# Convolution with max-pooling on one core: another order of warm-ups, weight turns and loads in the head

## The chip, the cores and the metric

The kernel runs on one core of one Trainium2 chip. The metric is the device time of a whole execution in microseconds. Profile times count from the first instruction of the profiled execution.

## What is computed

A 3x3 convolution with zero padding over 16 images of 64 channels and 64x64 pixels, 128 output channels, then the maximum over 2x2 blocks of pixels. Input, weights and output are fp32.

```python
x_pad = np.pad(x, ((0, 0), (0, 0), (1, 1), (1, 1)))
conv[b, co] += weight[co, ci, kh, kw] * x_pad[b, ci, kh:kh+h, kw:kw+w]   # over ci, kh, kw
output[b, c, i, j] = np.max(conv[b, c, 2*i:2*i+2, 2*j:2*j+2])
```

## The kernel before

**Tiles.** Two images at a time lie on the 128 partitions (2 x 64 channels). Every product in `taps` uses one image, so 64 partitions of input and a 64x128 weight, and products for the two images run in pairs. Eight pairs of images are split into two classes: four pairs "k" are cast to bf16 and multiplied as they are (`kx`); four pairs "w" are loaded in fp32 (`wx`) and enter as sums and differences of neighbouring rows. Each pair is cut into four chunks of 16 rows; unit i stands for chunk i % 4 of pair i // 4, and there are 16 units in each class. A unit gives 8 rows of the pooled output for two images.

**Two rows at once.** For each pair of output rows the kernel computes one PSUM tile `ta` and one `tb`. For class k: PA(i) fills `ta` (12 products with the weights D2 and G0), PB(i) fills `tb` (12 with D0 and G2). EV(i) copies `ta` to SBUF on ScalarE, MX(i) takes the maximum of the two into `tb` on VectorE, and PR(i) adds to `tb` the products of G1 with the row sums KS(i), which both rows share. OD(i) copies the odd columns on ScalarE, CM(i) takes the maximum with the even ones on VectorE and stores. For class w the parts are P2, P0 (into `ta`), SE (ScalarE puts minus `ta` into `tb`), P3, P1 (into `tb`) and ev, mx, od, cm; their inputs are the row operations E (`we`), Z (`wz`), Y (`wy`) and WS (`ws`). KS, WS and the first five E run on VectorE, Z and Y on GpSimd. There are four PSUM tiles of two banks each (`acc`), handed out by the list `free` in the order of the program.

**Weights.** `wraw` holds the raw weights. Seven blocks of them are needed with input channels on the partitions: D2 = g2-g1, G0, D0 = g0-g1, G2, GM, G1 and GP, with GM and GP half of g0+g2-g1 and half of g0+g2+g1. Each is made as a bf16 block of `wq` (VectorE or ScalarE), turned by four transposes on TensorE into a PSUM tile (TD2, TG0, ...; `turn`, line 148), and copied to `wt` (VD2, VG0, ...; `turn_out`, lines 161 to 167). GS, the sum g0+g2, runs on GpSimd.

**Order.** Nothing is scheduled automatically: each engine gets its instructions in the order of the strings HEAD, STEADY and TAIL, and does them in that order. `behind` adds a wait of one instruction for another; `on_gpsimd` lets a GpSimd operation wait for the last VectorE operation noted by `on_vector`.

**The head.** Before HEAD, eight products of zeros warm up TensorE (`zero`, line 135; two for each PSUM tile[...]). The loads go out from SyncE's queue: `wraw` and `kfirst` (the first 17 rows of the first k pair) at once, the first `wx` chunk behind the fourth warm-up, and after it `ksecond` (the next 16 rows). XO casts the odd rows of `kfirst` on VectorE, XE the even ones; X1 and X2 do the same for `ksecond` on ScalarE. The other three `wx` chunks wait for XO. The remaining rows of the first k pair are loaded from GpSimd's queue with a cast under way (`kload`, line 95), behind E.0. A tile in the set `unset` gets two products of zeros when SE first uses it.

Of the kernel before, what the change touches and what calls it, by code (L numbers as in the profile page):

```python
# [11 lines left out]
def kernel(  # L12
# [21 lines left out]
    nc = tc.nc  # L34
    FP32 = mybir.dt.float32
    BF16 = mybir.dt.bfloat16
    MAX = mybir.AluOpType.max
    ADD = mybir.AluOpType.add
    SUB = mybir.AluOpType.subtract

    B, CI, H, W = x.shape
# [18 lines left out]

    acc = [psum.tile([128, 2, R, W], FP32, name=f"acc_{i}") for i in range(4)]
    free = deque(range(4))
    unset = set()

# [3 lines left out]
    def behind(inst, other):  # L70
        if other is not None:
            tc.add_manual_dep(inst.ins, other.ins.name, SYNC, reason="order")

    def on_vector(inst):
        sbuf_op[0] = inst
        return inst

    def on_gpsimd(inst):
        behind(inst, sbuf_op[0])
        return inst  # L80


    def rows_of(p, lo, hi):
        return x[2 * p : 2 * p + 2].rearrange("b c h w -> (b c) h w")[:, lo:hi, :]

    def chunk(q):
        return (2 * R * q + (q > 0), min(H, 2 * R * (q + 1) + 1))
# [4 lines left out]
    def kload(j, lo, hi):  # L92
        if j not in kx:
            kx[j] = kx_pool.tile([128, H, W], BF16, name="kx")
        return nc.gpsimd.dma_start(out=kx[j][:, lo:hi, :], in_=rows_of(2 * j, lo, hi))  # L95

    def wload(i):
        j, q = divmod(i, NQ)
        lo, hi = chunk(q)
        return nc.sync.dma_start(  # L100
            out=wx[j % 2][:, lo + 1 : hi + 1, :], in_=rows_of(2 * j + 1, lo, hi)
        )
# [6 lines left out]
    klo2, khi2 = chunk(1)  # L109
    ksecond = const.tile([128, khi2 - klo2, W], FP32)  # L110
# [10 lines left out]
    D2, G0, D0, G2, GM, G1, GP = range(1, 29, 4)  # L121
    BLOCKS = {"D2": D2, "G0": G0, "D0": D0, "G2": G2, "GM": GM, "G1": G1, "GP": GP}
# [6 lines left out]
    g0, g1, g2 = wv[:, 0:3, :], wv[:, 3:6, :], wv[:, 6:9, :]  # L129

    def slots(m):
        return wq[:, m : m + 3, :]

    def zero(t, h):
        return nc.tensor.matmul(  # L135
            acc[t][:, h], zeros[:, 0:128], zeros, start=True, stop=True, skip_group_check=True
        )

    turned = {}

    def turn(m):
        t = free.popleft()
        turned[m] = t
        unset.add(t)
        tp = acc[t][:, 0].rearrange("p a b -> p (a b)").bitcast(BF16)
        lo, hi = BLOCKS[m] - 1, BLOCKS[m] + 3
        for j in range(lo, hi):
            nc.tensor.transpose(  # L148
                tp[:, (j - lo) * 128 : (j - lo + 1) * 128],
                wq[:, j : j + 2, :].rearrange("a b c -> a (b c)"),  # L150
                ident,
            )

    def turn_out(m):
        t = turned[m]
        free.append(t)
        lo, hi = BLOCKS[m] - 1, BLOCKS[m] + 3
        src = acc[t][:, 0].rearrange("p a b -> p (a b)").bitcast(BF16)[:, 0 : (hi - lo) * 128]
        dst = wt[:, lo:hi, :].rearrange("p a b -> p (a b)")
        if m == "GM":  # L160
            nc.scalar.mul(dst, src, 0.5)
        elif m == "GP":
            nc.vector.tensor_scalar_mul(out=dst, in0=src, scalar1=0.5)
        elif m in ("G0", "G1", "G2"):
            nc.scalar.copy(out=dst, in_=src)
        else:
            nc.vector.tensor_copy(out=dst, in_=src)
# [66 lines left out]
    def row_out(name, i):  # L234
        j, q = divmod(i, NQ)
        if (name, j) not in row:
            row[name, j] = row_pool.tile([128, HO, W], BF16, name=name)
        return row[name, j][:, q * R : (q + 1) * R, :]

    def row_in(t, first, pad):  # L240
        a = first + pad
        return t[:, a : a + 2 * R - 1 : 2, :]

    def row_op(engine, name, i, a, b, op):
        j, q = divmod(i, NQ)
        t, pad = (kx[j], 0) if name == "ks" else (wx[j % 2], 1)
        f = 2 * R * q
        return engine.tensor_tensor(  # L248
            out=row_out(name, i), in0=row_in(t, f + a, pad), in1=row_in(t, f + b, pad), op=op
        )  # L250

    def ks(i):
        on_vector(row_op(nc.vector, "ks", i, 0, 1, ADD))

    def ws(i):
        on_vector(row_op(nc.vector, "ws", i, 0, 1, ADD))

    def we(i):
        if i < 5:
            inst = on_vector(row_op(nc.vector, "we", i, 1, 0, SUB))  # L260
            if i == 0:
                behind(kload(0, chunk(2)[0], H), inst)
        else:
            on_gpsimd(row_op(nc.gpsimd, "we", i, 1, 0, SUB))

# [69 lines left out]
    def cast_rows(first):  # L335
# [3 lines left out]
        if first == 1:  # L339
            for i in range(1, NQ):  # L340
                behind(wload(i), inst)

    def cast_more(first):
        nc.scalar.copy(out=kx[0][:, klo2 + first : khi2 : 2, :], in_=ksecond[:, first::2, :])

# [2 lines left out]
        "g1": lambda: nc.scalar.copy(out=slots(G1), in_=g1),  # L348
        "g2": lambda: nc.scalar.copy(out=slots(G2), in_=g2),
        "D2": lambda: on_vector(nc.vector.tensor_sub(out=slots(D2), in0=g2, in1=g1)),  # L350
        "D0": lambda: on_vector(nc.vector.tensor_sub(out=slots(D0), in0=g0, in1=g1)),
        "GS": lambda: on_gpsimd(nc.gpsimd.tensor_tensor(out=gsum, in0=g0, in1=g2, op=ADD)),
        "GM": lambda: on_vector(
            nc.vector.tensor_sub(out=slots(GM), in0=gsum, in1=g1)
# [4 lines left out]
        "XO": lambda: cast_rows(1),  # L359
        "XE": lambda: cast_rows(0),  # L360
        "X1": lambda: cast_more(0),
        "X2": lambda: cast_more(1),
        "PA": pa, "PB": pb, "PR": pr, "P0": p0, "P1": p1, "P2": p2, "P3": p3,
        "KS": ks, "WS": ws, "E": we, "Z": wz, "Y": wy, "SE": seed,
        "EV": lambda i, h=None: evac(("k", i), h), "ev": lambda i, h=None: evac(("w", i), h),
        "MX": lambda i, h=None: rowmax(("k", i), h), "mx": lambda i, h=None: rowmax(("w", i), h),
# [3 lines left out]
    for m in BLOCKS:  # L370
        steps["T" + m] = lambda m=m: turn(m)
        steps["V" + m] = lambda m=m: turn_out(m)

    HEAD = """
        D2 g0 D0 g2 GS g1 TD2 VD2 TG0 VG0 XO TD0 VD0 TG2 VG2 TG1 VG1 XE GM PA.0 GP TGM VGM TGP
        KS.0 E.0 WS.0 PB.0 EV.0 X1 Z.0 Y.0 VGP P2.0 MX.0 SE.0 X2 PA.1 EV.1 WS.1 KS.1 E.1 PR.0
        P0.0 P3.0 Z.1 Y.1 OD.0 CM.0 P2.1 ev.0 PB.1 SE.1 mx.0 P0.1 P1.0 MX.1 P3.1 ev.1 od.0 PR.1
        WS.2 KS.2 E.2 Z.2 Y.2 OD.1 cm.0 CM.1 PA.2 EV.2 P2.2 PB.2 SE.2 mx.1 P1.1 P0.2 MX.2 P3.2
        od.1 ev.2 cm.1 E.3 KS.3 WS.3 Z.3 Y.3 PR.2 PA.3 OD.2 CM.2 P2.3 mx.2 EV.3 PB.3 SE.3 P1.2
# [12 lines left out]
    """  # L392
    FIRST, LAST = 4, 12

    for n in range(8):
        warm = zero(n // 2, n % 2)
        if n == 3:
            behind(wload(0), warm)
            nc.sync.dma_start(out=ksecond, in_=rows_of(0, klo2, khi2))
    kx[0] = kx_pool.tile([128, H, W], BF16, name="kx")  # L400

    def run(order):
# [44 lines left out]
```

## Time and profile before

| | us |
|---|---|
| median of 4 runs (107.57 to 108.78) | 107.98 |
| the profiled execution | 107.94 |
| its span, first to last instruction | 106.2 |
| TensorE busy | 98.9 |
| VectorE busy | 82.6 |
| ScalarE busy | 72.7 |
| GpSimd busy | 60.2 |

The span is that of one execution; the time of the same execution holds 1.7 us more. In the profile PE is TensorE, PEld its weight loads, DVE VectorE, ACT ScalarE, POOL GpSimd and SP SyncE; a letter q behind a name is the engine's queue. A line such as "L183" is the kernel's line, and since helpers issue most instructions, the tiles tell more than the lines: `acc<-kx,wt` at L183 is PA or PB, `acc<-we,wt` is P2, `acc<-ident,wq` at L148 a turn. The chain of waits goes back from the last instruction to what released each step. The timeline has, on each line, the start, the length, the engine, the line and operation, the tiles and their shape, how many instructions are merged, and in brackets the idle time before them and what ended it.

### The profile page before, as it was taken

The numbers are of one execution on the slowest core, as the hardware profiler recorded it, in microseconds if no ns is written. First come the engines' busy times: TensorE is split into PE (matmuls) and PEld (weight loads), VectorE is DVE, ScalarE is ACT, GpSimd is POOL, SyncE is SP. The second block draws the span as 40 slices with busy tenths as digits, with TensorE's granted clock in tenths as the row PEclk, the third lists the DMA queues.
The fourth block names the chain that finished last, engine by engine and source line by source line (L and its number), as shares of the span: only waits on it lengthen the run. The fifth ranks groups of instructions, "written<-read, shape, count | busy, mean of one in ns | idle before, by whom it ended". The sixth has DMA issues, their size and how long they took to land.

```text
span 106.2 us, 2338 instructions
## 1 busy us (share of the span) xinstructions
PE 98.9 (93%) x900; PEld 45.4 (43%) x900; DVE 82.6 (78%) x113; ACT 72.7 (68%) x92; POOL 60.2 (57%) x69
## 2 busy tenths in 40 slices
PE   5989989999999999999999999999999999999810
PEld 2445434444444444444444444444444444455400
DVE  1489989969797869698787868687978868686950
ACT  4557985676767678767867676787777676775820
POOL 6205674823519494958567594949294765835000
PEclk9999999999999999999999999999999999999995
DMA  2998996899986768999956589999968412232052
GB/s 63 346 342 275 318 208 146 213 267 328 277 301 177 223 158 158 215 331 201 336 210 193 194 190 158 237 319 208 364 220 176 150 68 102 99 105 99 0 198 99
DMA packets 12475, 21.96 MB, mean 207 GB/s; under 512 B 944, under 2 KB 9136, under 8 KB 12464
## 3 DMA queue, kind: packets, MB, share of 16 engines
q1 hardware_dynamic: 11312, 18.03, 53.3%
q0 software_dynamic: 1008, 3.65, 19.3%
q8 instruction: 7, 0.11, 0.4%
q10 hardware_dynamic: 144, 0.13, 0.4%
q14 instruction: 4, 0.03, 0.1%
HBM read 17.07 MB, written 8.39 MB: 240 GB/s over the span
## 4 chain that ended last, share of the span: by engine, by line
PE 80%; DVE 10%; DMA 4%; issue 1%; ACT 1%; SPq 0%; DVEq 0%
PE acc L183 80%; DVE acc L299 6%; DMA kfirst<-in_x_dram 4%; DVE ws L248 2%; DVE o L318 1%; DVE we L248 1%; ACT od L304 1%; PE acc L148 1%; DVE kx L337 0%; SPq L105 0%; DVE ks L248 0%; DVEq L299 0%
## 5 line engine op out<-in xcount | busy, mean ns | idle before, releaser
L183 PEld LDWEIGHTS <-wt 64*128 64x128 bf16 x864 | 42.6, 94 | 51.6 <-issue 1.1
L299 DVE TENSOR_TENSOR acc<-acc,ev 128x1024 f32<-128x1024 f32 (+1 forms) x34 | 39.5, 1165 | 12.2 <-PE acc L183 11.9
L183 PE MATMUL acc<-kx,wt 64*128 64x504 bf16 (+3 forms) x384 | 46.2, 373 | 0.5 <-DVE kx L337 0.5
L286 ACT COPY ev<-acc 128x1024 f32<-128x1024 f32 (+1 forms) x34 | 32.5, 963 | 12.5 <-PE acc L183 11.0
L248 POOL TENSOR_TENSOR wz<-wx 128x512 bf16<-128x512 f32 x16 | 20.4, 1276 | 30.1 <-DVE ws L248 23.2
L304 ACT COPY od<-acc 128x512 f32<-128x512 f32 x32 | 18.8, 587 | 11.6 <-PE acc L183 11.5
L318 DVE TENSOR_TENSOR o<-acc,od 128x512 f32<-128x512 f32 x32 | 21.9, 690 | 3.6 <-ACT od L304 3.6
L248 POOL TENSOR_TENSOR wy<-wx 128x512 bf16<-128x512 f32 x16 | 20.4, 1274 | 0.0
L295 ACT ACTIVATE acc<-acc 128x1024 f32<-128x1024 f32 x16 | 16.1, 1008 | 1.3 <-PE acc L183 0.8
L248 POOL TENSOR_TENSOR we<-wx 128x512 bf16<-128x512 f32 x11 | 14.1, 1280 | 0.1
L183 PE MATMUL acc<-ws,wt 64*128 64x504 bf16 (+1 forms) x96 | 13.0, 377 | 0.4 <-DVE acc L299 0.4
L183 PE MATMUL acc<-we,wt 64*128 64x504 bf16 (+1 forms) x96 | 13.0, 377 | 0.3 <-DVE we L248 0.3
L183 PE MATMUL acc<-ks,wt 64*128 64x504 bf16 (+1 forms) x96 | 13.0, 377 | 0.1
L183 PE MATMUL acc<-wy,wt 64*128 64x504 bf16 (+1 forms) x96 | 13.0, 377 | 0.0
L183 PE MATMUL acc<-wz,wt 64*128 64x504 bf16 (+1 forms) x96 | 13.0, 377 | 0.0
L248 DVE TENSOR_TENSOR ws<-wx 128x512 bf16<-128x512 f32 x16 | 12.2, 762 | 0.0
L248 DVE TENSOR_TENSOR ks<-kx 128x512 bf16<-128x512 bf16 x16 | 6.7, 416 | 0.0
L95 POOL DMA_DIRECT2D kx<-in_x_dram x7 | 4.2, 594 | 3.7 <-DVE we L248 3.7
L135 PE MATMUL acc<-zeros 128*128 128x512 bf16 x8 | 3.6, 631 | 1.2 <-DVE zeros L112 1.2
L248 DVE TENSOR_TENSOR we<-wx 128x512 bf16<-128x512 f32 x5 | 3.4, 683 | 0.0
L350 DVE TENSOR_TENSOR wq<-wraw 128x192 bf16<-128x192 f32 x1 | 0.5, 500 | 2.6 <-DMA wraw<-in_weight_dram 2.6
L135 PEld LDWEIGHTS <-zeros 128*128 128x128 bf16 x8 | 1.0, 141 | 2.8 <-issue 1.7
(26 smaller groups left out, 17.0 us busy)
## 6 DMA issues: line engine op xcount, KB each, us to landing
out_dram<-o SPq DMA_DIRECT2D x31, 256.0 KB, 3.3
wx<-in_x_dram SPq DMA_DIRECT2D x8, 512.0 KB, 6.0
wx<-in_x_dram SPq DMA_DIRECT2D x4, 544.0 KB, 6.0
kx<-in_x_dram POOLq DMA_DIRECT2D x4, 496.0 KB, 8.2
wx<-in_x_dram SPq DMA_DIRECT2D x4, 480.0 KB, 4.9
kx<-in_x_dram POOLq DMA_DIRECT2D x3, 528.0 KB, 8.0
kfirst<-in_x_dram SPq DMA_DIRECT2D x1, 544.0 KB, 4.7
ksecond<-in_x_dram SPq DMA_DIRECT2D x1, 512.0 KB, 5.6
```

What stands on the lines that cost most here:

```text
L95: return nc.gpsimd.dma_start(out=kx[j][:, lo:hi, :], in_=rows_of(2 * j, lo, hi))
L135: return nc.tensor.matmul(acc[t][:, h], zeros[:, 0:128], zeros, start=True, stop=True, skip_group_check=True)
L148: nc.tensor.transpose(tp[:, (j - lo) * 128 : (j - lo + 1) * 128], wq[:, j : j + 2, :].rearrange("a b c -> a (b c)"), ident,)
L183: nc.tensor.matmul(dst[:, half, i0:i1, o0:o1], wt[lo : lo + CI, m0 + kw - half, :], rows(lo, i0, i1, c0, c1), start=start and kw == 1, sto ...
L248: return engine.tensor_tensor(out=row_out(name, i), in0=row_in(t, f + a, pad), in1=row_in(t, f + b, pad), op=op)
L286: nc.scalar.copy(out=ev[g][:, halves(h)], in_=acc[ta[g]][:, halves(h)])
L295: nc.scalar.mul(acc[t], acc[ta["w", i]], -1.0)
L299: nc.vector.tensor_tensor(out=t, in0=t, in1=ev[g][:, halves(h)], op=MAX)
L304: nc.scalar.copy(out=od[g][:, halves(h)], in_=acc[tb[g]][:, halves(h), :, 1::2])
L318: nc.vector.tensor_tensor(out=o, in0=acc[tb[g]][:, s, :, 0::2], in1=od[g][:, s], op=MAX)
L350: "D2": lambda: on_vector(nc.vector.tensor_sub(out=slots(D2), in0=g2, in1=g1)),
```

## The change

Six warm-up products are issued instead of eight, so the fourth PSUM tile gets none, and all four tiles begin in `unset`. `ksecond` is loaded behind D0 instead of behind the fourth warm-up. The casting load of the first k pair goes out behind KS.0 instead of E.0. The turns of G1 and GP share one PSUM tile, a bank each, and stand behind PB.0; G1's had been before PA.0, GP's before PB.0. G1's copy to `wt` is made by VectorE instead of ScalarE. In HEAD, GM stands before XE, and E.1 and KS.1 before WS.1. STEADY and TAIL stay as they are.

```diff
-    unset = set()
+    unset = set(range(4))
...
+    def turned_cols(m):
+        lo, hi = BLOCKS[m] - 1, BLOCKS[m] + 3
+        tp = acc[turned[m]][:, int(m == "GP")].rearrange("p a b -> p (a b)").bitcast(BF16)
+        return lo, hi, tp[:, 0 : (hi - lo) * 128]
+
     def turn(m):
-        t = free.popleft()
-        turned[m] = t
-        unset.add(t)
-        tp = acc[t][:, 0].rearrange("p a b -> p (a b)").bitcast(BF16)
-        lo, hi = BLOCKS[m] - 1, BLOCKS[m] + 3
+        turned[m] = turned["G1"] if m == "GP" else free.popleft()
+        unset.add(turned[m])
+        lo, hi, tp = turned_cols(m)
...
     def turn_out(m):
-        t = turned[m]
-        free.append(t)
-        lo, hi = BLOCKS[m] - 1, BLOCKS[m] + 3
-        src = acc[t][:, 0].rearrange("p a b -> p (a b)").bitcast(BF16)[:, 0 : (hi - lo) * 128]
+        if m != "G1":
+            free.append(turned[m])
+        lo, hi, src = turned_cols(m)
...
-        elif m in ("G0", "G1", "G2"):
+        elif m in ("G0", "G2"):
             nc.scalar.copy(out=dst, in_=src)
...
     def ks(i):
-        on_vector(row_op(nc.vector, "ks", i, 0, 1, ADD))
+        inst = on_vector(row_op(nc.vector, "ks", i, 0, 1, ADD))
+        if i == 0:
+            behind(kload(0, chunk(2)[0], H), inst)
...
-            inst = on_vector(row_op(nc.vector, "we", i, 1, 0, SUB))
-            if i == 0:
-                behind(kload(0, chunk(2)[0], H), inst)
+            on_vector(row_op(nc.vector, "we", i, 1, 0, SUB))
...
+    def load_second(inst):
+        behind(nc.sync.dma_start(out=ksecond, in_=rows_of(0, klo2, khi2)), inst)
...
-        "D0": lambda: on_vector(nc.vector.tensor_sub(out=slots(D0), in0=g0, in1=g1)),
+        "D0": lambda: load_second(
+            on_vector(nc.vector.tensor_sub(out=slots(D0), in0=g0, in1=g1))
+        ),
...
-        D2 g0 D0 g2 GS g1 TD2 VD2 TG0 VG0 XO TD0 VD0 TG2 VG2 TG1 VG1 XE GM PA.0 GP TGM VGM TGP
-        KS.0 E.0 WS.0 PB.0 EV.0 X1 Z.0 Y.0 VGP P2.0 MX.0 SE.0 X2 PA.1 EV.1 WS.1 KS.1 E.1 PR.0
+        D2 g0 D0 g2 GS g1 TD2 VD2 TG0 VG0 XO TD0 VD0 TG2 VG2 GM XE PA.0 TGM GP KS.0 PB.0 VGM
+        EV.0 TG1 TGP E.0 WS.0 X1 P2.0 VG1 Z.0 Y.0 VGP SE.0 MX.0 X2 PA.1 EV.1 E.1 KS.1 WS.1 PR.0
...
-    for n in range(8):
+    for n in range(6):
         warm = zero(n // 2, n % 2)
         if n == 3:
             behind(wload(0), warm)
-            nc.sync.dma_start(out=ksecond, in_=rows_of(0, klo2, khi2))
```

## The prediction

> **What bounds the kernel now.** I read the busy shares first, then the chain of waits, then each engine's timeline over the first 16 us, the stretch that the change touches. The first line of the page says which engine sets the length:
>
> ```profile
> PE 98.9 (93%) x900; PEld 45.4 (43%) x900; DVE 82.6 (78%) x113; ACT 72.7 (68%) x92; POOL 60.2 (57%) x69
> ```
>
> TensorE is busy for 93% of the span, so the question is what it does when it isn't computing output. The chain of waits shows where that is (start, length, what):
>
> ```profile
> 1.19 4.74 DMA kfirst<-in_x_dram
> ...
> 5.96 0.44 DVE kx L337
> ...
> 6.44 1.39 PE acc L183 x12
> 7.83 0.56 PE acc L148 x8
> 8.39 1.42 PE acc L183 x12
> ...
> 9.90 1.23 DVE acc L299
> 11.14 1.84 DVE ws L248
> 12.98 0.34 DVE ks L248
> 13.31 0.61 DVE we L248
> ...
> 13.97 77.55 PE acc L183 x720
> ```
>
> From 13.97 us on, 77.55 us are unbroken TensorE products. A change in the head is therefore worth how much earlier or later P2.1 starts, the `we` product at 13.97. Before it, two things are on the path: `kfirst` landing at 5.93 with its first cast (XO) behind it, which releases PA.0 at 6.44; and VectorE's row of MX.0, WS.1, KS.1, E.1, which releases P2.1. The timeline of TensorE:
>
> ```profile
> 1.19 3.60 PE L135 MATMUL acc<-zeros 128*128 128x512 bf16 x8 [1.19 <-DVE zeros L112]
> 4.58 1.36 PE L148 MATMUL acc<-ident,wq 128*128 128x128 bf16 x20
> 6.44 1.39 PE L183 MATMUL acc<-kx,wt 64*128 64x512 bf16 x12 [0.50 <-DVE kx L337]
> ...
> 13.97 0.82 PE L183 MATMUL acc<-we,wt 64*128 64x512 bf16 x6 [0.28 <-DVE we L248]
> ```
>
> Five turns (20 transposes) stand before PA.0 and end at 5.94, half a microsecond before the data: they are free there. Ends are modelled, so I count from start to start: a group of six conv products takes 0.65 (11.57 to 12.22 to 12.87), so P2.1 could have begun at 13.52 and is 0.45 late, not 0.28. VectorE's row behind that wait, and the GpSimd row beside it:
>
> ```profile
> 11.05 1.92 DVE L248 TENSOR_TENSOR ws<-wx 128x512 bf16<-128x512 f32 x1
> ```
>
> ```profile
> 11.14 1.28 POOL L248 TENSOR_TENSOR wy<-wx 128x512 bf16<-128x512 f32 x1
> ```
>
> WS.1 takes 1.92 where its like, WS.0, took 0.69. It ends 0.56 after GpSimd's Y.0 does (12.98 against 12.42).
>
> [...] the 4096-byte packets of `ksecond`, issued at 3.48, begin only at 5.99, once `kfirst` has landed. [...] the warm-ups start every 0.43 us, the conv products later in pairs every 0.215, and the transposes go from 0.107 to 0.056 apart at about 4.7, 3.5 us after the first product. (The page's clock row shows full grant even there.)
>
> **The change, part by part.**
>
> *Two warm-ups fewer.* Removes 2 x 0.43 = 0.85 us of TensorE ahead of the first turn. That turn then waits for D2, which ends at 4.20: it starts near 4.35 instead of 4.58. Worth nothing on the path, as PA.0 waits for XO at 6.39; the work that hides it is the `kfirst` transfer. If that landed at 5.3 or earlier, it would be worth up to 0.2. Its possible price, a later full rate, is a rival below.
>
> *Second chunk's load behind D0.* D0 ends at 4.61, so its issue (0.43) runs to about 5.07 instead of 3.92. Its packets wait in the queue until 5.99 anyway; descriptors of `wraw` were moving 0.6 us after their issue ended (1.13 to 1.75), so these are ready by 5.7. Landing stays near 9.12, and X1, which reads it, starts at 9.59. For the same reason `kfirst` gains nothing: none of `ksecond` moves before it lands. SyncE waits for D0 with only the three `wx` loads behind, which wait for XO until 6.41 anyway. Zero; bounds -0.1 to +0.2 on X1, whose product PA.1 has slack here.
>
> *Turns G1 and GP moved behind PB.0.* G1's four leave a free place and come to a bound one; GP's four stay bound. A change between turns and products costs about 0.10 (last transpose start 8.17 plus 0.056, yet PB.0 at 8.32). Before: PA.0, 8 turns, PB.0, P2.0 at 6.44, 7.77, 8.32, 9.63. After: PA.0 6.44; GM's turns 7.77; PB.0 at 7.77 + 4 x 0.056 + 0.10 = 8.09; turns at 8.09 + 1.31 + 0.10 = 9.50; P2.0 at 9.50 + 8 x 0.056 + 0.10 = 10.05. That is **+0.42**.
>
> *G1's copy from ScalarE to VectorE.* ScalarE loses about 0.5 us (1.56 for three), in a place where it then waits 1.33 for GM. VectorE gains 0.42, the time of its like VD2, in the queue between WS.0 and MX.0, with VGP (0.42), KS, E and MX.0 behind it. WS.0 ends at 9.47; the copy waits for the turn: 9.91 to 10.33, VGP to 10.67, MX.0 10.59 to 11.82 instead of 11.14. PA.1 takes the PSUM tile that VGP frees: it would follow P2.0 at 10.70 and starts at 10.72, **+0.02**. PR.0, which waits for MX.0, is due at 12.02: 0.2 of slack.
>
> *GM ahead of XE, E.1 and KS.1 ahead of WS.1.* XE ends near 7.5 instead of 7.12; PB.0 needs it at 8.09. GM is ready at 7.05. E.1 now comes right after MX.0: start 11.74, and Y.0 is then nearly done. Y.0 moves up because the casting load no longer sits between WS.0 and Z.0: that load (0.70) goes out behind KS.0 at 8.27 instead of behind E.0 at 8.88, so Z.0 starts at WS.0's end, 9.50, and Y.0 runs 10.74 to 12.0. E.1 ends at 12.0 + 0.56 = 12.57. P2.1 needs it at 13.97. The wait of **0.45 is gone**; what is late next is EV.1 on ScalarE (about 13.3), which frees P2.1's tile, with 0.7 to spare, then the product line itself. The earlier casting load may share engines with the `wx` loads (landed 12.89, 14.09); WS.2 reads them at 17.27. Zero; bounds -0.1 to +0.1.
>
> Sum: P2.1 at 10.72 + 1.30 + 3 x 0.65 = 13.97, against 13.97. 0.42 + 0.02 - 0.45 is **zero** within 0.05. The profiled execution took 107.94 (span 106.2 and 1.74 around it), 0.04 under the median of the four runs, 107.98. I forecast 107.9.
>
> **Rivals.**
>
> *A late full rate (slower).* With eight warm-ups TensorE is busy without a break from 1.19 to 5.94[...]. With six it stops near 3.8, resumes at 4.35, stops near 5.5 and waits for PA.0 until 6.44. [...] It decides as soon as full rate comes after 6.44. [...] Against: the idle stretches are short.
>
> *VectorE's queue becomes the bound.* MX.0 has 0.2 us of slack before PR.0. If the two copies start later, or E.1 is blocked longer, P2.1 slips: +0.2 to +0.6, 108.1 to 108.5. Against: all durations come from like rows.
>
> *The data come earlier than in this profile.* Most packets of `kfirst` are in by 4.7; a few end 1.2 later. If they don't lag in other executions, PA.0 is bound by the turns: then G1's 0.22 and the earlier start (0.23) count: -0.45, 107.5, and 107.1 with a little from the loads. Against: it is the one landing I can see.
>
> **How the numbers follow.** The sum holds: 0.60, at 107.5 to 108.3. Late rate: 0.20, of which a part stays within 1%. VectorE's queue: 0.10. Earlier data: 0.10. One per cent, 1.08 us, is about what a measurement of this kernel can tell from no change. Faster by that needs more than any case here gives, but for unseen gains in the loads: 0.06. Slower by it: 0.19, the late rate and a little of the queue. Same: 0.75. The range 107.1 to 109.0 takes in the sum, the earlier data, the queue and the near part of the late rate.
>
> **What would show it.** Right: in the chain, `kfirst` and XO to PA.0 near 6.44; L151 x4 between PA.0 and PB.0 and x8 behind PB.0; `we` of E.1 ending near 12.6; P2.1 within 0.15 of 13.97 with no VectorE wait; `ksecond` landing near 9.1. Wrong: PA.0 or PB.0 longer than 1.4 (late rate), a wait of PR.0 for MX.0, or PA.0 well before 6.4.

## The result, and the profile after

The changed kernel takes 108.56 us (median of 44 runs, 107.99 to 110.26) where the kernel before, measured beside it, takes 107.85 (63 runs). The ratio is 1.0055, with a 95% interval from 1.0039 to 1.007: 0.6 us slower, inside the range but clear of no change. Its profiled execution took 108.59 with a span of 106.8, against 107.94 and 106.2.

The chain of waits of the changed kernel (start, length, what) has another head:

```profile
0.74 2.99 DMA wraw<-in_weight_dram
...
3.75 0.50 DVE wq L355
4.25 0.42 DVE wq L357
...
4.69 5.95 DMA ksecond<-in_x_dram
...
10.67 0.63 ACT kx L349
...
11.34 80.80 PE acc L185 x750
```

`kfirst` and XO are gone from it. In their place stands D0 (the `wq` operation at L357), and behind it the load of the second chunk, from 4.69 to 10.64, then X1, then PA.1 at 11.34, from where TensorE doesn't stop for 80.80 us. Before, that load had gone out at 3.48 and landed at 9.12. TensorE's timeline of the changed kernel:

```profile
5.97 1.39 PE L185 MATMUL acc<-kx,wt 64*128 64x512 bf16 x12 [0.25 <-DVE kx L339]
7.29 0.40 PE L151 MATMUL acc<-ident,wq 128*128 128x128 bf16 x4
7.62 1.47 PE L185 MATMUL acc<-kx,wt 64*128 64x512 bf16 x12
9.03 0.62 PE L151 MATMUL acc<-ident,wq 128*128 128x128 bf16 x8
9.58 0.82 PE L185 MATMUL acc<-we,wt 64*128 64x512 bf16 x6
11.34 1.47 PE L185 MATMUL acc<-kx,wt 64*128 64x512 bf16 x12 [0.93 <-ACT kx L349]
...
14.57 0.83 PE L185 MATMUL acc<-we,wt 64*128 64x512 bf16 x6
```

Here the six lines down to PA.1 are PA.0, GM's turn, PB.0, the turns of G1 and GP, P2.0 and PA.1. PA.1 begins 1.76 after P2.0 instead of 0.65, and the bracket names X1. P2.1 at 14.57 no longer waits for VectorE, but stands 0.60 later than before: the whole difference of the two spans. P2.1's start is the landing at 10.64, 0.70 for X1 and the start of PA.1, and 3.23 for PA.1 and the three groups behind it. PA.0 is not on this path: it began at 5.97 instead of 6.44, `kfirst` having landed at 5.46 instead of 5.93, and that gained nothing here.

That the second chunk moves slowly can be seen in the transfer rates. Each line is a stretch in us and its length, the busy time and count of TensorE's products, its weight loads, VectorE, ScalarE and GpSimd, then the clock, the DMA engines' share, and GB/s as the last number. First the kernel before:

```profile
6.00:6.50 0.50, 0.06 (x2) 0.06 (x4) 0.50 (x2) 0.50 (x2) 0.00 (x0) 1.00 0.96 327
6.50:7.00 0.50, 0.50 (x6) 0.25 (x8) 0.50 (x2) 0.37 (x1) 0.00 (x0) 1.00 1.00 373
7.00:7.50 0.50, 0.50 (x10) 0.20 (x4) 0.50 (x3) 0.00 (x0) 0.00 (x0) 1.00 0.84 320
```

Then the changed kernel in the same stretches:

```profile
6.00:6.50 0.50, 0.50 (x6) 0.29 (x7) 0.50 (x2) 0.38 (x1) 0.00 (x0) 1.00 1.05 196
6.50:7.00 0.50, 0.50 (x9) 0.24 (x5) 0.50 (x3) 0.00 (x0) 0.00 (x0) 1.00 0.67 257
7.00:7.50 0.50, 0.50 (x8) 0.21 (x4) 0.50 (x3) 0.00 (x0) 0.00 (x0) 1.00 1.00 255
```

By the trace's packet records the second chunk begins at 5.87 before and at 5.91 after, while the last packets of the first w chunk are still moving. From there the core's transfers together run at 196 to 257 GB/s instead of 320 to 373. In the first of these stretches the DMA engines are no less busy than before (1.05 against 0.96): packets take longer, the first nine of the chunk 0.36 to 1.60 us each, where eight of nine had taken 0.16. Later the engines stand partly idle: from 7.5 to 9.0 their share is 0.48 to 0.66, at 156 to 180 GB/s. The kernel before has slow stretches too, 246 and 180 GB/s from 8.0 to 9.0, but there the chunk is nearly in.

### The profile page after: what moved, and what is told of

Same layout as the page of the kernel before. It is cut to its first block, busy times and chain, and to the rows that moved or that the text cites. A ratio compares the mean times of both kernels' runs of the same rounds, so it can differ in the third digit from the quotient of the medians.

```text
span 106.8 us, 2330 instructions
## 1 busy us (share of the span) xinstructions
PE 98.7 (92%) x898; PEld 49.0 (46%) x898; DVE 82.1 (77%) x114; ACT 72.3 (68%) x91; POOL 60.1 (56%) x69
## 4 chain that ended last, share of the span: by engine, by line
PE 80%; DMA 8%; DVE 6%; ACT 1%; issue 1%; DVEq 0%
PE acc L185 80%; DMA ksecond<-in_x_dram 6%; DVE acc L301 5%; DMA wraw<-in_weight_dram 3%; DVE o L320 1%; ACT kx L349 1%; ACT od L306 1%; DVE wq L355 0%; DVE wq L357 0%; DVEq L301 0%
## 5 line engine op out<-in xcount | busy, mean ns | idle before, releaser
L185 PEld LDWEIGHTS <-wt 64*128 64x128 bf16 x864 | 46.4, 94 | 48.0 <-issue 2.0
L250 DVE TENSOR_TENSOR ws<-wx 128x512 bf16<-128x512 f32 x16 | 10.9, 684 | 0.0
L135 PE MATMUL acc<-zeros 128*128 128x512 bf16 x6 | 2.7, 630 | 1.2 <-DVE zeros L112 1.2
L151 PEld LDWEIGHTS <-wq 128*128 128x128 bf16 x28 | 1.9, 108 | 2.1 <-issue 1.8
L151 PE MATMUL acc<-ident,wq 128*128 128x128 bf16 x28 | 2.3, 238 | 0.5 <-DVE wq L355 0.5
```

The costliest lines, as they stand in the source:

```text
L135: return nc.tensor.matmul(acc[t][:, h], zeros[:, 0:128], zeros, start=True, stop=True, skip_group_check=True)
L151: nc.tensor.transpose(tp[:, (j - lo) * 128 : (j - lo + 1) * 128], wq[:, j : j + 2, :].rearrange("a b c -> a (b c)"), ident,)
L185: nc.tensor.matmul(dst[:, half, i0:i1, o0:o1], wt[lo : lo + CI, m0 + kw - half, :], rows(lo, i0, i1, c0, c1), start=start and kw == 1, sto ...
L250: return engine.tensor_tensor(out=row_out(name, i), in0=row_in(t, f + a, pad), in1=row_in(t, f + b, pad), op=op)
```

## The experiments

All ratios are to the kernel before, measured beside each kernel. "PA.0 to PB.1" is the distance of the two starts in the profile; it leaves out when PA.0 happened to begin. The last column says when the load of the second chunk went out and landed.

| kernel | ratio (95% interval) | PA.0 to PB.1 | second chunk |
|---|---|---|---|
| before | 1 | 8.19 | 3.48, 9.12 |
| changed | 1.0055 (1.0039 to 1.007) | 9.25 | 4.69, 10.64 |
| load back | 1.0020 (0.9988 to 1.0052) | 8.51 | 3.48, 9.21 |
| before, load late | 1.0047 (1.0025 to 1.0069) | 8.48 | 4.96, 10.00 |
| changed, eight warm-ups | 1.0059 (1.0038 to 1.008) | 9.41 | 4.89, 11.01 |
| changed, load behind D2 | 1.0054 (1.0037 to 1.0071) | 8.86 | 4.17, 10.33 |
| before, E.1 first | 0.9997 (0.9975 to 1.0019) | 8.11 | 3.48, 8.97 |
| the same, casting load earlier | 0.9977 (0.996 to 0.9994) | 7.81 | 3.48, 8.82 |
| the same, measured again | 0.9968 (0.9944 to 0.9992) | 7.82 | 3.48, 9.20 |
| the same, six warm-ups | 0.9971 (0.995 to 0.9992) | 7.81 | 3.48, 8.70 |
| load back, eight warm-ups | 1.0021 (1.0005 to 1.0036) | 8.51 | 3.48, 9.48 |
| load behind 6th warm-up | 1.0021 (1.0005 to 1.0036) | 8.50 | 3.96, 9.31 |
| load behind 7th of eight | 1.0055 (1.0037 to 1.0074) | 9.13 | 4.39, 10.60 |
| load behind 8th of eight | 1.0055 (1.0034 to 1.0075) | 9.10 | 4.82, 10.96 |

Where the landing is early, the time of the profiled execution less the start of PA.0 follows the third column: 101.50 us before, 101.40 with E.1 first, 101.12 and 101.10 with the casting load earlier too. In the five kernels with the changed order and a late landing it doesn't: there PB.1 starts 4.57 or 4.58 behind the landing, wherever PA.0 stood (5.97 to 6.43), and the time is 97.90 to 97.95 us more than the landing. The landing alone sets their time.

### One part undone, one part alone

The load goes out behind the fourth warm-up again, all else as changed:

```diff
         if n == 3:
             behind(wload(0), warm)
+            nc.sync.dma_start(out=ksecond, in_=rows_of(0, klo2, khi2))
```

> The changed kernel with one part undone: the load of the second chunk goes out behind the fourth warm-up again. Theory A (the load is issued too late: the first w chunk is drained before its descriptors are there, the queue stands empty, X1 and with it PA.1 wait): the load lands at 9.0 to 9.4, PA.1 follows P2.0 without a wait for ScalarE, P2.1 starts near 13.5 to 13.9 instead of 14.57, and the time is 107.5 to 107.9, ratio to before 0.995 to 1.001. Theory B (the turns behind the products are what costs): 108.4 to 108.7, as the changed kernel. Theory C (two warm-ups fewer, a late full rate): also 108.4 to 108.7.

The converse, the kernel before with the load behind D0 alone:

```diff
+        "D0": lambda: load_second(
+            on_vector(nc.vector.tensor_sub(out=slots(D0), in0=g0, in1=g1))
+        ),
...
             behind(wload(0), warm)
-            nc.sync.dma_start(out=ksecond, in_=rows_of(0, klo2, khi2))
```

> The kernel before with one part of the change alone: the load of the second chunk behind D0. Theory A: it lands at 10.4 to 10.9 instead of 9.12, PA.1 waits for X1 until about 11.3 (1.05 later), of which the 0.45 that P2.1 waited for E.1 hides a part: P2.1 near 14.6, time 108.4 to 108.6, ratio 1.005 to 1.007, as much as the whole change. Theory B and C: lands at 9.1 to 9.4, ratio 0.998 to 1.002.

The chain of the kernel before with the late load alone is that of the changed kernel:

```profile
4.96 5.04 DMA ksecond<-in_x_dram
...
10.02 0.63 ACT kx L347
...
10.69 80.97 PE acc L183 x750
```

That part alone costs 0.47% where the whole change costs 0.55%, with intervals that overlap almost wholly; its landing at 10.00 and its 108.34 us are a little earlier and faster than theory A expected. Undoing it takes the landing back to 9.21 and P2.1 to 13.75. The time falls to 108.10 us, not as far as theory A expected. The interval of these fourteen runs reaches both the kernel before and the changed one; the two kernels below with an early load, at 1.0021, lie clear of the changed kernel's interval. The next lines, TensorE of the kernel with the load back, say what was left over:

```profile
9.51 0.82 PE L185 MATMUL acc<-we,wt 64*128 64x512 bf16 x6
10.50 1.47 PE L185 MATMUL acc<-kx,wt 64*128 64x512 bf16 x12 [0.17 <-DVE wt L165]
...
13.75 0.81 PE L185 MATMUL acc<-we,wt 64*128 64x512 bf16 x6
```

PA.1 still stands 0.99 behind P2.0 and not 0.65, now because of GP's copy on VectorE (L165).

### The warm-ups

Eight of them in the changed kernel (`range(8)` in place of `range(6)`):

> The changed kernel with eight warm-ups. Theory A: nothing moves, 108.4 to 108.7, ratio to before 1.004 to 1.007, X1 still released by the load at about 10.6. Theory C: the transposes reach their short distance earlier and the products of PA.0 and PB.0 shorten; 107.7 to 108.1.

Nothing moved: 1.0059. With the load back as well, so that the load doesn't hide them:

> The changed kernel with the second chunk's load behind the fourth warm-up again and eight warm-ups: what is left of the change are the turns and the order on VectorE and GpSimd. By the forecast's sum 0.42 + 0.02 - 0.45: 107.7 to 107.9, ratio 0.998 to 1.001. If the two warm-ups fewer cost something in other executions than the profiled one, it is 0.1 to 0.4 faster than the kernel with the load back and six warm-ups (108.1); if not, the two are the same within 0.15.

1.0021, the same as the 1.0020 with six. It is not the "zero" of the forecast's sum either: its interval begins at 1.0005, so what is left of the change costs about 0.2 us.

### How late is too late

The load behind D2, behind the sixth warm-up, and (with eight of them) behind the seventh and the eighth:

```diff
+        if n == 5:
+            load_second(warm)
```

> The changed kernel with the load of the second chunk behind D2 (ends near 4.2) instead of D0 (near 4.65): issued about 0.4 earlier. Theory A, if what counts is whether the descriptors come before the queue runs empty (near 5.5 to 6.0): most of the delay goes, landing at 9.2 to 10.0, time 107.7 to 108.2. If the landing simply moves with the issue, it lands near 10.2 and the time falls by 0.4 at most, 108.1 to 108.2. Theory B and C: 108.4 to 108.7.

> The changed kernel with the second chunk's load behind the sixth warm-up: SyncE is released near 3.95, between the 3.48 of the kernel before and the 4.17 of the load behind D2. If the landing depends on how long before the first w chunk's end (5.5 to 6.0) the load goes out: landing between 9.2 and 10.2, time 107.9 to 108.3. If only an issue straight behind the w chunk's is free of the gap: landing 10.2 or later, time 108.4 to 108.6.

> The changed kernel with eight warm-ups and the second chunk's load behind the seventh (SyncE released near 4.38), nothing on VectorE waited for. If the time of issue decides (3.96 was early enough, 4.17 was not): landing 10.0 to 11.0, ratio to before 1.004 to 1.007. If the wait for VectorE's D2 or D0 was what made the load late: landing 9.2 to 9.6, ratio 1.001 to 1.003.

> As with the seventh, behind the eighth warm-up (near 4.81, as late as behind D0 in the changed kernel). Time of issue: landing 10.3 to 11.2, ratio 1.004 to 1.008, no faster than behind the seventh. The wait for VectorE: landing 9.2 to 9.6, ratio 1.001 to 1.003.

The table shows a step. Issued at 3.48 or 3.96, the chunk lands between 8.70 and 9.48; at 4.17 or later, between 10.00 and 11.01. The times of these four fall into the same two groups, 1.0021 and 1.0054 to 1.0055. With the 97.9 us from landing to time, the medians of the five late kernels, 108.42 to 108.56, put a typical landing at 10.5 to 10.6 (an estimate), whether the load went out at 4.17 or at 4.89. The step is in the landing; the rate has a middle: behind the sixth warm-up 298 to 314 GB/s were moved from 6.0 to 7.5. Whether SyncE was released by TensorE or by VectorE made no difference: 10.60 and 10.96 behind the warm-ups, 10.33 and 10.64 behind D2 and D0. Half of theory A fell with the load behind D2: going out 0.5 earlier than behind D0 gained nothing in the median time, though the issue ended at 4.50, 1.4 before the first packet.

### A full queue in between

Here 512 KB of the second w chunk are put ahead of the late load, to keep the queue full:

```diff
             behind(wload(0), warm)
+            wload(1)
...
-            for i in range(1, NQ):
+            for i in range(2, NQ):
```

> The changed kernel, with the second w chunk's load (512 KB) straight behind the first, ahead of the second k chunk's load, which stays behind D0. Theory A (the queue runs empty in between): the transfer rate from 6.0 to 7.5 stays above 300 GB/s, as in the kernel before, and the second k chunk lands no more than 0.3 later than the 10.64 of the changed kernel, perhaps earlier, although 512 KB more are ahead of it. If a load issued so late is slow in itself (six microseconds from issue to landing on top of what is ahead of it): landing at 11.8 or later, time 0.8 or more above the changed kernel's.

> The changed kernel with the second w chunk's load ahead of the second k chunk's late one, looked at again, because the first look fell on the slowest of its eight executions (109.97, median 109.19). If the queue running empty is the whole loss, 512 KB at the 340 GB/s of a full queue move the landing from the 9.2 of an early load to 10.7: 10.5 to 11.0 in this look. If the late load also starts slowly behind a full queue: 11.3 or later, with a stretch of 1 us or more under 290 GB/s after 8.0.

The medians are 109.19 and 109.03, ratios 1.011 and 1.0105. The profiled executions are the slowest of eight and the second slowest of fourteen, so their landings, 12.05 and 11.62, are at the late end. In the first, 368, 373 and 397 GB/s were moved from 6.0 to 7.5, no less than in the kernel before (327, 373 and 320): the queue was full there, as theory A wanted. But from 8.0 to 10.5, with the late load under way, the second shows 369, 270, 279, 287 and 295. At 340 GB/s, the mean of the three stretches of the kernel before, the 512 KB would have put the landing near 10.7 (an estimate; 10.2 to 11.0, by the early landings of the table). The medians, less 97.9, put a typical one at 11.1 to 11.3 (an estimate). So an empty queue is probably not the whole of it, but the margin is small, and the slow stretch was seen in these two executions alone. What slows the late load isn't settled here.

### Where the 0.45 of E.1 went

The kernel before with one edit, and then with the casting load moved as in the change:

```diff
-        EV.0 X1 Z.0 Y.0 VGP P2.0 MX.0 SE.0 X2 PA.1 EV.1 WS.1 KS.1 E.1 PR.0
+        EV.0 X1 Z.0 Y.0 VGP P2.0 MX.0 SE.0 X2 PA.1 EV.1 E.1 KS.1 WS.1 PR.0
```

> The kernel before with one part alone: E.1 and KS.1 ahead of WS.1. By the forecast's sum this part alone takes away the 0.45 that P2.1 waits: P2.1 starts 7.08 after PA.0 instead of 7.53, time 107.3 to 107.5, ratio 0.995 to 0.997. Rival: the wait only passes to another releaser (EV.1, which frees P2.1's tile, or the first w chunks landing), ratio 0.998 to 1.001.

With E.1 first alone, TensorE shows:

```profile
12.96 0.81 PE L183 MATMUL acc<-we,wt 64*128 64x512 bf16 x6
13.99 1.26 PE L183 MATMUL acc<-kx,wt 64*128 64x512 bf16 x10 [0.22 <-DVE o L318]
```

P2.1 starts 7.08 after PA.0 (5.88), exactly as forecast. But PB.1 behind it comes 1.03 later, not 0.65: it waits for CM.0 (`o`), which frees its PSUM tile. VectorE's line says why CM.0 is late:

```profile
10.48 1.92 DVE L248 TENSOR_TENSOR we<-wx 128x512 bf16<-128x512 f32 x1
```

Now E.1, in the place behind MX.0, takes the 1.92 that WS.1 had taken there, and WS.1 behind it 0.68 (12.66). All behind them is as late as it was: CM.0 starts 7.38 after PA.0 (13.26) where it had started 7.40 after it (13.84). 0.38 of the 0.45 passed to the next wait. With the casting load behind KS.0 as well:

> The kernel before with E.1 first and the casting load behind KS.0. If the earlier casting load costs nothing, as the forecast had it: the same as with E.1 first alone, within 0.1. If it takes transfer time from the w chunks or delays the row operations on VectorE: 0.1 to 0.4 slower than that.

> The kernel before with E.1 first and the casting load behind KS.0, measured again, since its first ratio was 0.9977 with an interval up to 0.9994: the same, 0.996 to 0.999; if the first was chance, 0.999 to 1.001.

E.1 takes 1.44 and 1.62 in the two profiles, and PB.1 is 0.08 or 0.09 late. The changed kernel has the same casting load, and there Y.0 ended 5.74 after PA.0 (11.71) instead of 5.98 (12.42); that it ended sooner here too is an estimate. From PA.0 to PB.1 it is 7.81 and 7.82 instead of 8.19. TensorE in the second:

```profile
6.08 1.39 PE L183 MATMUL acc<-kx,wt 64*128 64x512 bf16 x12
...
13.16 0.81 PE L183 MATMUL acc<-we,wt 64*128 64x512 bf16 x6
13.90 1.47 PE L183 MATMUL acc<-kx,wt 64*128 64x512 bf16 x12
```

This version beats both kernels: 107.54 and 107.57 us, 0.9977 and 0.9968. The earlier casting load was not without effect, as the forecast had it: 0.30 of the 0.38 came with it. The intervals of the times with and without it overlap, but only the kernels with it can be told from the kernel before. Six warm-ups on top:

> The kernel before with E.1 first and the casting load behind KS.0, and six warm-ups instead of eight. Theory C in small (the first turns run at half rate for longer, and PA.0 comes later in some executions): 0.1 to 0.4 slower than with eight (107.54). The forecast's view (hidden behind the first chunk): the same within 0.15, ratio 0.996 to 0.999.

0.9971: no difference.

### Two turns in one tile

VectorE of the changed kernel:

```profile
9.76 0.42 DVE L169 COPY wt<-acc 128x512 bf16<-128x512 bf16 x1 [0.69 <-PE acc L151]
```

G1's turn begins at 9.03, so its four transposes are done near 9.42 (0.167 to the last start and 0.22 for it). The copy is released near 9.65, when GP's last transpose ends (9.43 and 0.22). To test whether the shared tile does this, the copy is placed between the two turns, in the kernel with the load back and eight warm-ups:

```diff
-        EV.0 TG1 TGP E.0 WS.0 X1 P2.0 VG1 Z.0 Y.0 VGP SE.0 MX.0
+        EV.0 TG1 E.0 WS.0 VG1 TGP X1 P2.0 Z.0 Y.0 VGP SE.0 MX.0
```

> The kernel with the load back and eight warm-ups, with G1's copy placed in the program between the turns of G1 and GP. Theory D (the two turns share a PSUM tile, and the waits are set for the whole tile, so the copy of G1 waits for GP's turn too): now GP's turn must wait for G1's copy instead. The copy starts about 0.4 after G1's first transpose instead of 0.73, GP's turn about 0.9 after it instead of 0.23, and P2.0 comes 0.6 to 0.7 later from PA.0 than the 3.61 there. If the wait for both turns had another reason (VectorE busy): the copy still starts about 0.7 after G1's first transpose and nothing else moves.

TensorE of that kernel:

```profile
9.26 0.40 PE L151 MATMUL acc<-ident,wq 128*128 128x128 bf16 x4
10.24 0.38 PE L151 MATMUL acc<-ident,wq 128*128 128x128 bf16 x4 [0.59 <-DVE wt L169]
10.56 0.82 PE L185 MATMUL acc<-we,wt 64*128 64x512 bf16 x6
```

GP's turn now waits for G1's copy (`wt` at L169) and begins 0.98 after G1's. P2.0 is 4.36 behind PA.0 (6.20) instead of 3.61, and its one run took 108.47 us. Whichever comes first in the program, the other waits, although they are in different banks: in this program the waits are set for the whole tile. No run gives each turn a tile of its own.

## Why the prediction was wrong

The step that failed is "Second chunk's load behind D0 ... Landing stays near 9.12 ... Zero; bounds -0.1 to +0.2 on X1, whose product PA.1 has slack here." The landing moved by 1.5, from 9.12 to 10.64. I had taken the 0.6 us between the end of `wraw`'s issue and its first packet, seen when nothing else was moving, as the time that any load needs to be ready. The first packet did come at 5.91, where it was before (5.87, not the 5.99 of the forecast, and behind the first w chunk, which the forecast leaves out of the queue); the rate behind it was what fell. PA.1's "slack" was 0.06 in the kernel before: P2.0's six products make room near 10.28 (9.63 and 0.65), and X1 ended at 10.22. With the forecast's own PA.1 at 10.72 it is 0.5; a landing 1.5 later is more than either. Undone, the load makes the changed kernel 0.3% faster; alone, it makes the kernel before 0.5% slower. Why a load issued 1.2 later than before moves so slowly stays open.

Point by point:

- *Warm-ups, zero:* right, with six and eight the same in the changed kernel and in two others. The late-rate rival did not happen in the changed kernel's profile: PA.0 and PB.0 took 1.39 and 1.47 as before. By the clock records of all the traces full rate came between 4.77 and 6.12 with six warm-ups (seven traces) and between 4.26 and 6.57 with eight (ten): with the idle stretches which the rival feared, the latest is no later than with eight. What decides when it comes, no run shows.
- *Turns, +0.42:* right. P2.0 is 3.61 behind PA.0 instead of 3.19.
- *G1's copy, +0.02 on PA.1:* wrong, 0.34 (0.99 against 0.65 with the load back). I let the copy start once its own transposes were done; it waits for both turns in the tile. In the changed kernel the load's wait covers this and the turns' 0.42.
- *E.1 first, -0.45:* right for P2.1, but I named EV.1 as what is late next. It is CM.0, for PB.1: without the earlier casting load 0.38 came back there. In the changed kernel E.1 started at 12.34 instead of 11.74, when its w chunk had landed behind the late load; P2.1 didn't wait for it.
- *Casting load, zero within 0.1:* wrong, a gain of 0.30 (8.11 to 7.81) when E.1 stands first.
- *The data come earlier:* true of the data, in part of PA.0. In all sixteen profiles other than the one I had, `kfirst` landed between 5.24 and 5.68, not at 5.93, but PA.0 began between 5.88 and 6.43.

PA.0 can be late without late data, as TensorE shows in the kernel with E.1 first, the earlier casting load and six warm-ups, where `kfirst` had landed at 5.50:

```profile
4.33 2.11 PE L148 MATMUL acc<-ident,wq 128*128 128x128 bf16 x20 [0.39 <-DVE wq L350]
6.37 1.39 PE L183 MATMUL acc<-kx,wt 64*128 64x512 bf16 x12
```

Full rate came only at 6.12, the turns took 2.11 instead of 1.36, and PA.0 stood behind them without waiting for the data. With eight warm-ups it was the same in three kernels where full rate came at 5.81, 5.89 and 6.57. The median of the kernel before, 107.85, less the 101.50 between its PA.0 and its time, puts a typical PA.0 at 6.35, and the three kernels like this one (101.1) give 6.4 to 6.5 (estimates). So the forecast's 6.44 was typical, though the late data that it rested on were not seen again.

With the load back the parts add up: 0.42 for the turns and 0.34 for the shared tile, less 0.45, make 0.31, and from PA.0 to PB.1 it is 8.51 instead of 8.19. In the changed kernel they don't count one by one: they would have put PA.1 at 10.57 (9.58 and 0.99), and the load put it at 11.34. The time fell into the forecast's range because that was wide, not because the sum held: the sum, 0.42 and 0.02 against 0.45, was close enough to zero that any missed wait had to decide the sign.

## What to carry to other kernels

A load that is queued behind others is not safe to issue later just because it has to queue: here 1.2 later at the issue (3.48, 4.69) was 1.5 later at the landing (9.12, 10.64). Measure the landing, above all where its reader has little slack, as X1 had for PA.1 (0.06). Before adding up what parts of a change cost, ask which of them lie on the path that remains: behind a late landing the others don't count (here the time was 97.90 to 97.95 more than the landing in all five kernels). When a wait is to be removed by reordering, look for the next tile that the reordered queue frees, not only for the next operand (0.38 of 0.45 came back here). Two results in one PSUM tile can make each reader wait for both writers, even where they lie in different banks, as here (0.34 on PA.1).

## What was not expected of the hardware

A load of 512 KB issued at 3.96 or before landed by 9.48; issued 0.21 later, at 4.17, it landed at 10.33, with the same loads ahead of it. The six profiles of loads issued at 4.17 or later (without the filler) show 10.00 to 11.01, and the rate from 6.0 to 7.5 at about 150 to 280 GB/s. The order of issue was kept: the changed kernel's first w chunk, issued at 3.12, landed at 7.76, its second k chunk, issued at 4.69, at 10.64. But the order says nothing about the rate (196 to 257 GB/s there from 6.0 to 7.5).

TensorE fell back to half rate after a wait of 1.84 us in one profile, the second one with the filler. The line below them, in the form explained above, is the stretch for which its clock stood at half, 0.50:

```profile
12.31 2.35 PE L185 MATMUL acc<-kx,wt 64*128 64x512 bf16 x12 [1.84 <-ACT kx L349]
14.42 1.52 PE L185 MATMUL acc<-ks,wt 64*128 64x512 bf16 x6
```

```profile
12.75:16.17 3.42, 3.42 (x20) 1.47 (x18) 1.23 (x3) 2.16 (x4) 1.33 (x2) 0.50 0.81 186
```

The twelve products take 2.35 instead of 1.47, and the six behind them start 1.28 before the next group, not 0.65. This execution's time is 99.6 us more than its landing, not 97.9. In the first profile of the same kernel a longer wait (2.21) left the rate alone.

The clock record of the second profile shows full rate from 5.93 to 12.75, half until 16.17 and full behind it; PA.1 had begun 0.44 before the rate fell. In the other sixteen traces full rate lasts 98.99 or 102.40 without a break. Why the rate fell behind the wait of 1.84 and not behind that of 2.21, no run shows.

The clock records also settle a remark in the prediction. That of the kernel before begins at 4.72, where the transposes close up from 0.107 to 0.056 apart; for the time ahead of it the trace holds no entry, and the profile's clock row counts such time as full grant.
